# Moving two input norms to GpSimd on transposed data, in a hybrid encoder layer

## The chip, the cores and the metric

The kernel runs on one core of one Trainium2 chip. The metric is the device time of one execution in microseconds (us); lower is better. A core has a matmul engine (PE, TensorE), which loads its stationary operand with separate instructions (PEld), and three engines for element-wise work: DVE (VectorE), ACT (ScalarE) and POOL (GpSimd). SP (SyncE) issues most of the DMAs. Each engine takes its instructions in order.

## The reference

One layer of an encoder on 512 tokens of width 1024 in float32, with a memory of 256 tokens. Only the start of it matters here:

```
h = rmsnorm(x, pre_mix_g)                       # x * rsqrt(mean(x^2) + eps) * g, by row
aq, ak, av, hq, hf_fwd, hf_bwd, hi, hg = split_columns(h @ w_in, IN_SPLITS)
rec = hgrn2_group(hq, hf_fwd, hf_bwd, hi, hg, ...)     # 4 heads, a gated recurrence
...
m = rmsnorm(mem, mem_norm_g)
x = x + rmsnorm(memory_cross_attention(h, m, ...), ...)
```

Behind it come the grid attention on aq, ak and av, an output projection, the cross-attention into m, and a gated MLP with a small convolution. Each of the two norms above is a factor r by row (1/rms) and a gain g by column.

## The kernel before, in words

All matrix products are float32 made of three products of rounded parts: each operand is split into a part hi (rounded to the matmul's format, ACT writes it) and a remainder lo (DVE writes it, or POOL for 14 units), and `mm3` (L134) does hi·hi, hi·lo and lo·hi, lines 135 to 137. The weights come as 132 units of 128x1024, each loaded by SP (L110), cast by ACT (L102, out `wh`) and subtracted by DVE (L103, out `wl`). There are two buffers for raw units and four for split ones, so a load waits until the subtraction two units before it has been done, and a cast until PE has finished with the unit four before it. `unit` takes one and has up to three more issued ahead.

The order is written by hand as Python generators. `weave` advances that stream whose cost so far, divided by its share, is the smallest. Within this order a compile-time planner places the instructions on each engine by its own estimate of when their inputs will be there; each engine then runs its list in order. `tc.issue_after(i)` puts the instructions of a block that run on the engine of `i` behind `i`.

The start runs so. x comes twice: transposed (`xt`, 8 chunks of 128 features by 512 tokens) and by rows (`xr`). The first projection (the recurrence's values, L365) and head 0's three projections work on the raw transposed x times the gain (`split_x`, L335 and L336, into `raw_act`), as r is not known yet. ACT squares the rows (L378), POOL makes r (L153, L154), POOL writes four diagonal matrices of it (L382), PE multiplies them with ones (L385), and ACT copies the result (L387) to `r_bc`, which holds r along the tokens on every partition. Head 0's results are multiplied by `r_bc` on DVE (L435). Meanwhile `normalize` makes the normalised activation `hT`, chunk by chunk: DVE writes x·g·r (L392), ACT casts it and DVE subtracts (L102 and L103 with out `big`).

From there on everything reads `hT`. `mix_projections` begins with the memory's norm: loads of the gain and of the memory's rows on POOL's queue, squares on ACT (L188), r on POOL (L153, L154), scaling on DVE (L170). Then it does the gate projection (`put_sg`), heads 1 and 2 (`hgrn_in`), the memory's 16 transposes (`mem_turn`, L179, with four casts and four subtractions), keys and values, queries, and head 3. It is woven with `cores`, the recurrence of heads 0 to 2, whose first step is a sum on DVE (L486) and a matmul (L489), followed by level after level of ACT copies (L496), matmuls (L499) and DVE multiplies (L525). The shares are 100 and `CORE_SHARE` = 53, in which a step of the gate projection is 6 matmuls and costs 6 x 0.216 = 1.296. Large buffers (`big`) come from one pool of 16.

Of the kernel before, what the change touches and what calls it, by code (L numbers as in the profile page):

```python
# [18 lines left out]
P = 128  # L19
D = 1024  # L20
T = 512
NB = T // P
KC = D // P
M = 256
MB = M // P
# [6 lines left out]
TURN_STEP, MEM_TURN, UP_TURN = 0, (0, 4), (0, 2)  # L32
POOL_UNITS = frozenset(range(28, 42))
CORE_SHARE = 53.0
WARM = 4
LEVELS = (1, 2, 4, 8, 16, 32, 64)
ASK = 3
MIX_ORDER = (0, 2, 3, 1)
# [34 lines left out]
def layer(tc, io, out):  # L73
    nc = tc.nc
    ctx = ExitStack()
    pool = lambda name, **k: ctx.enter_context(tc.tile_pool(name=name, **k))
    const = pool("const", bufs=1)
# [20 lines left out]
    def tmp4(shape, dt=F32):  # L98
        return t4.tile(shape, dt, name="tmp4", tag="tmp4")

    def split(hi, lo, src, eng=None):
        nc.scalar.copy(hi, src)  # L102
        (eng or nc.vector).tensor_sub(lo, src, hi.bitcast(F32))  # L103
# [35 lines left out]
    def blk(b):  # L139
        return slice(b * P, (b + 1) * P)  # L140
# [4 lines left out]
    def gains(*names, eng=None):  # L145
        g = big([P, 2, D])
        for i, name in enumerate(names):
            (eng or nc.gpsimd).dma_start(g[:, i, :], rows_bc(io[name], D))
        return [g[:, i, :] for i in range(len(names))]

    def rstd_of(ss, n, width):
        r = small()
        nc.gpsimd.tensor_scalar(r[:, :n], ss, 1.0 / width, EPS, op0=ALU.mult, op1=ALU.add)  # L153
        last_pow[0] = nc.gpsimd.tensor_tensor(out=r[:, :n], in0=r[:, :n], in1=nhalf[:, :n], op=ALU.pow).ins  # L154
        return r
# [13 lines left out]
    def scale_rows(xb, r, g, h, c):  # L169
        nc.vector.scalar_tensor_tensor(out=h[:, half(c)], in0=xb[:, half(c)], scalar=r, in1=g[:, half(c)],  # L170
                                       op0=ALU.mult, op1=ALU.mult)

    def turn_in(h, act, b, tags, before=None):
        for c in range(2):
            if before:
                before(c)
            o = bank(tags[c]).rearrange("p (k n) -> p k n", k=4)
            for k in range(4):
                nc.tensor.transpose(o[:, k, :], h[:, blk(c * 4 + k)], ident)  # L179
            hi, lo = act.hi, act.lo  # L180
            if len(hi) == 2:
                split(hi[c][:, :, blk(b)], lo[c][:, :, blk(b)], o)
            else:
                split(hi[0][:, c * 4:c * 4 + 4, blk(b)], lo[0][:, c * 4:c * 4 + 4, blk(b)], o)

    def row_rstd(xb, h):
        ss = small()
        nc.scalar.activation(h, xb, ACT.Square, accum_out=ss[:, 0:1])  # L188
        return rstd_of(ss[:, 0:1], 1, D)[:, 0:1]
# [57 lines left out]
    def proj_tm(act, tags, use, n=512):  # L247
        o = [bank(t) for t in tags]
        nk = 1024 // n
        for j in range(8 // nk):  # L250
            w = unit(nk)
            for b in range(len(tags)):
                for k in range(nk):
                    kc = nk * j + k
                    mm3(o[b][:, :n], act.get(kc, blk(b)), (w[0][:, k, :], w[1][:, k, :]), kc == 0, kc == 7)
                if kc == 7:
                    use(b, o[b])
                yield 3 * nk * MM * n / 512
# [39 lines left out]
            pass  # L298

    ident = const.tile([P, P], F32, name="ident")  # L300
    gcol = const.tile([P, KC], F32, name="gcol")
    ones = const.tile([P, P], F32, name="ones")
    nhalf = const.tile([P, 16], F32, name="nhalf")
    warm = tmp2()
    xt = [big([P, 4, T]) for _ in range(2)]
    nc.scalar.dma_start(gcol, io["gx"])
    nc.gpsimd.memset(ones, 1.0)
    nc.vector.memset(warm[:, :256], 0.0)
    nc.gpsimd.memset(nhalf, -0.5)

    def load_xt(kc, n):
        nc.sync.dma_start(xt[kc // 4][:, kc % 4:kc % 4 + n, :], io["xt"][:, kc:kc + n, :])
# [15 lines left out]
    raw_act = new_act()  # L328

    after = []  # L330

    def split_x(kc):
        src = xt[kc // 4][:, kc % 4, :]
        hi, lo = raw_act.get(kc, slice(0, T))
        cast = nc.scalar.mul(hi, src, gcol[:, kc:kc + 1]).ins  # L335
        rest = nc.vector.scalar_tensor_tensor(out=lo, in0=src, scalar=gcol[:, kc:kc + 1], in1=hi.bitcast(F32),  # L336
                                              op0=ALU.mult, op1=ALU.subtract).ins
        return cast, rest
# [11 lines left out]
    v_ps = [bank(t) for t in "soso"]  # L350
    xr = room_x()
    ws = []
    for j in range(4):
# [7 lines left out]
        for k in range(2):  # L361
            kc = 2 * j + k
            for a, w in ((0, wh), (0, wl), (1, wh)):
                for b in range(NB):
                    nc.tensor.matmul(v_ps[b], raw_act.get(kc, blk(b))[a], w[:, half(k)],  # L365
                                     start=kc == 0 and a == 0 and w is wh, stop=kc == 7 and a == 1)
# [3 lines left out]
    ident_r = const.tile([P, P], F32R, name="ident_r")  # L370
    nc.vector.tensor_copy(ident_r, ident)
    taken[0] = 4
    for _ in range(2):
        issue()

    rx = const.tile([P, 2 * NB], F32, name="rx")
    for b in range(NB):
        nc.scalar.activation(tmp4([P, D]), xr[b], ACT.Square, accum_out=rx[:, b:b + 1])  # L378
    r = rstd_of(rx[:, :NB], NB, D)
    diag_r = tmp2((P, NB, P), tag="th")  # L380
    for b in range(NB):
        nc.gpsimd.tensor_scalar(diag_r[:, b, :], ident, r[:, b:b + 1], None, op0=ALU.mult)  # L382
    r_ps = bank("c")
    for b in range(NB):
        nc.tensor.matmul(r_ps[:, blk(b)], ones, diag_r[:, b, :], start=True, stop=True)  # L385
    r_bc = big([P, T])
    nc.scalar.copy(r_bc, r_ps)  # L387
    hT = new_act()

    def normalize(kc):  # L390
        t = tmp2()
        nc.vector.scalar_tensor_tensor(out=t, in0=xt[kc // 4][:, kc % 4, :], scalar=gcol[:, kc:kc + 1], in1=r_bc,  # L392
                                       op0=ALU.mult, op1=ALU.mult)
        split(*hT.get(kc, slice(0, T)), t)

    masks = const.tile([P, len(LEVELS), P], U8, name="masks")
    masks_f = tmp4([P, len(LEVELS), P])
# [29 lines left out]
    sg_box, heads, qkv, rec_done = [], {}, {}, [0]  # L427

    def put_v(b, o):
        nc.scalar.mul(v[:, b, :], o, r[:, b:b + 1])  # L430

    def scaled(put):
        def use(o):
# [15 lines left out]
    def hgrn_in(h, between=(), raw=False):  # L449
        qk = big([P, 2, 2, T])  # L450
        tt = big([P, 2048])
        q = tmp2(tag="tq")

        def put_q(z):
            nc.scalar.activation(q, z, ACT.Sigmoid)
            nc.vector.tensor_mul(q, z, q)

        def put_f(d):
            def put(z):
                f = tt[:, d * T:(d + 1) * T]  # L460
                k = qk[:, 1, d, :]
                nc.scalar.activation(f, z, ACT.Sigmoid)
                nc.scalar.activation(k, z, ACT.Sigmoid, scale=-1.0)
                nc.vector.tensor_scalar(f, f, oml[:, d, h:h + 1], lb[:, d, h:h + 1], op0=ALU.mult, op1=ALU.add)
# [162 lines left out]
    kv = {}  # L627

    def mem_norm():
        g_mem, = gains("mem_norm_g")  # L630
        kv["rows"] = big([P, MB, D])
        for b in range(MB):
            m = kv["rows"][:, b, :]
            nc.gpsimd.dma_start(m, io["mem"][blk(b), :])
            r = row_rstd(m, tmp4([P, D]))
            for c in range(2):
                scale_rows(m, r, g_mem, m, c)

    def mem_turn():
        kv["m"] = Act([big([P, 8, M], F32R)], [big([P, 8, M], F32R)])  # L640
        for b in range(MB):
            turn_in(kv["rows"][:, b, :], kv["m"], b, "bb")

    def mix_projections():
        mem_norm()
        yield from proj_tm(hT, tm_tags, put_sg)
        yield from hgrn_in(1)
        yield from hgrn_in(2)
        mem_turn()
        yield from proj_tm(hT, tm_tags, put_kv, 256)  # L650
        late = []
        yield from proj_tm(hT, tm_tags, lambda b, z: late.append(lambda: put_qn(b, z)))
        yield from hgrn_in(3, late)

    def cores():
        for h in range(3):
            yield from hgrn_core(h)

    for b in range(NB):
        put_v(b, v_ps[b])  # L660
    for i, _ in enumerate(hgrn_in(0, raw=True)):
        if i < KC:
            normalize(i)
    weave((mix_projections(), 100.0), (cores(), CORE_SHARE))

    kT, vv, qT = qkv["kT"], qkv["vv"], qkv["qT"]
# [340 lines left out]
```

## Time and profile before

| | |
|---|---|
| runs, us | 849.77, 849.8, 851.0; median 849.8 |
| profiled execution | 851.05 us, of it the span 849.3 us |
| mean granted clock of PE | 0.996 |
| busy in the span | PE 828.8, DVE 526.6, ACT 401.1, POOL 95.9 us |
| PE's longest stops | 5.60 us before 61.17, 1.55 before 206.91, 1.41 before 254.19, 1.37 before 6.38 |
| time to landing, weight units | 3.3 us, median of 131 |

The page lists each engine's busy time, then the span in 40 slices, then the DMA queues, then the chain of work that ended last, then the costliest groups of instructions. A line of a group reads: source line, engine, operation, out<-in with sizes, count, and then busy us, mean ns of one, and the engine's idle time ahead of them with what ended it. In a listing in order of time the first column is the start, the second the duration; in brackets stands the idle time before it and what released it.

### The profile page before, as it was taken

The numbers are of one execution on the slowest core, as the hardware profiler recorded it, in microseconds if no ns is written. First come the engines' busy times: TensorE is split into PE (matmuls) and PEld (weight loads), VectorE is DVE, ScalarE is ACT, GpSimd is POOL, SyncE is SP. The second block draws the span as 40 slices with busy tenths as digits, with TensorE's granted clock in tenths as the row PEclk, the third lists the DMA queues.
The fourth block names the chain that finished last, engine by engine and source line by source line (L and its number), as shares of the span: only waits on it lengthen the run. The fifth ranks groups of instructions, "written<-read, shape, count | busy, mean of one in ns | idle before, by whom it ended". The sixth has DMA issues, their size and how long they took to land.

```text
span 849.3 us, 11048 instructions
## 1 busy us (share of the span) xinstructions
PE 828.8 (98%) x4304; PEld 702.9 (83%) x4304; DVE 526.6 (62%) x799; ACT 401.1 (47%) x710; POOL 95.9 (11%) x128
## 2 busy tenths in 40 slices
PE   8979999999999999999999999999999999999996
PEld 6868888887889888888888998888888888888885
DVE  5598497969997774854443865555555557722224
ACT  6563345445878884644543643333333335511121
POOL 0311100224243301300001300000000000000001
PEclk9999999999999999999999999999999999999999
DMA  9722202122222224252312242223233332322212
GB/s 323 232 76 75 74 25 87 51 76 75 75 75 91 78 81 175 75 174 75 100 50 75 76 135 98 95 94 100 100 100 99 100 100 79 101 96 97 100 49 100
DMA packets 24756, 83.52 MB, mean 98 GB/s; under 512 B 3264, under 2 KB 3904, under 8 KB 24704
## 3 DMA queue, kind: packets, MB, share of 16 engines
q1 hardware_dynamic: 22752, 77.44, 27.5%
q0 software_dynamic: 1232, 4.46, 1.7%
q10 hardware_dynamic: 720, 0.92, 0.3%
q8 instruction: 34, 0.56, 0.3%
q14 instruction: 18, 0.15, 0.1%
HBM read 80.71 MB, written 2.10 MB: 98 GB/s over the span
## 4 chain that ended last, share of the span: by engine, by line
PE 87%; DVE 6%; DMA 3%; ACT 2%; issue 1%; POOL 0%; POOLq 0%; DVEq 0%; ACTq 0%
PE ps_b L135 9%; PE ps_b L136 9%; PE ps_b L137 9%; PE ps_s L137 6%; PE ps_s L135 6%; PE ps_s L136 6%; PE ps_o L135 6%; PE ps_o L137 6%; PE ps_o L136 6%; PE ps_c L135 4%; PE ps_c L136 4%; PE ps_c L137 4%; PE ps_c L499 3%; DMA raw<-in_w_dram 2%; PE ps_o L717 2%; DVE big L525 1%
## 5 line engine op out<-in xcount | busy, mean ns | idle before, releaser
L103 DVE TENSOR_TENSOR wl<-raw,wh 128x1024 fp32r<-128x1024 f32 x114 | 139.4, 1223 | 219.7 <-ACT wh L102 219.6
L102 ACT CAST wh<-raw 128x1024 fp32r<-128x1024 f32 x128 | 134.6, 1052 | 243.5 <-PE ps_o L137 80.5
L135 PE MATMUL ps_b<-big,wh 128*128 128x512 f32 (+1 forms) x320 | 118.0, 369 | 0.0
L136 PE MATMUL ps_b<-big,wh 128*128 128x512 f32 (+1 forms) x320 | 116.6, 364 | 0.0
L137 PE MATMUL ps_b<-big,wl 128*128 128x512 f32 (+1 forms) x320 | 116.5, 364 | 0.0
L137 PEld LDWEIGHTS ps_b<-big,wl 128*128 128x128 f32 x320 | 60.3, 188 | 9.3
L135 PEld LDWEIGHTS ps_b<-big,wh 128*128 128x128 f32 x320 | 60.4, 189 | 9.1
L136 PEld LDWEIGHTS ps_b<-big,wh 128*128 128x128 f32 x320 | 60.4, 189 | 8.9
L163 POOL TENSOR_SCALAR small<-small 128x1 f32<-128x1 f32 x40 | 14.0, 350 | 440.6 <-ACT tmp L194 421.7
L135 PE MATMUL ps_s<-wh,big 128*128 128x512 f32 (+1 forms) x140 | 53.8, 384 | 0.0
L137 PE MATMUL ps_s<-wh,big 128*128 128x512 f32 (+1 forms) x140 | 53.4, 382 | 0.0
L136 PE MATMUL ps_s<-wl,big 128*128 128x512 f32 (+1 forms) x140 | 52.9, 378 | 0.0
L525 DVE TENSOR_TENSOR big<-big 128x512 f32<-128x512 f32 x64 | 49.8, 786 | 2.7 <-PE ps_c L499 1.6
L135 PE MATMUL ps_o<-wh,big 128*128 128x512 f32 (+1 forms) x124 | 47.5, 383 | 0.0
L137 PE MATMUL ps_o<-wh,big 128*128 128x512 f32 (+1 forms) x124 | 47.3, 381 | 0.0
L136 PE MATMUL ps_o<-wl,big 128*128 128x512 f32 (+1 forms) x124 | 47.1, 380 | 0.0
L103 DVE TENSOR_TENSOR big<-ps_o,big 128x512 fp32r<-128x512 f32 x52 | 35.8, 688 | 15.9 <-ACT big L102 15.5
L103 POOL TENSOR_TENSOR wl<-raw,wh 128x1024 fp32r<-128x1024 f32 x14 | 33.9, 2424 | 57.9 <-ACT wh L102 49.2
L102 ACT CAST big<-ps_o 128x512 fp32r<-128x512 f32 x52 | 30.4, 585 | 19.9 <-PE ps_o L814 7.5
L135 PE MATMUL ps_b<-wh,big 128*128 128x512 f32 x92 | 36.6, 398 | 0.0
L136 PE MATMUL ps_b<-wl,big 128*128 128x512 f32 x92 | 36.1, 392 | 0.0
L137 PE MATMUL ps_b<-wh,big 128*128 128x512 f32 x92 | 36.0, 391 | 0.0
(246 smaller groups left out, 1891.7 us busy)
## 6 DMA issues: line engine op xcount, KB each, us to landing
raw<-in_w_dram SPq DMA_DIRECT2D x131, 512.0 KB, 3.3
big<-in_x_dram SPq DMA_DIRECT2D x8, 512.0 KB, 7.3
big<-in_xt_dram SPq DMA_DIRECT2D x3, 512.0 KB, 8.0
big<-in_mem_dram POOLq DMA_DIRECT2D x2, 512.0 KB, 9.4
out_dram<-big SPq DMA_DIRECT2D x4, 256.0 KB, 2.1
out_dram<-big ACTq DMA_DIRECT2D x3, 256.0 KB, 2.1
big<-in_xt_dram SPq DMA_DIRECT2D x2, 256.0 KB, 3.4
raw<-in_w_dram SPq DMA_DIRECT2D x2, 256.0 KB, 4.0
```

Source lines behind the costliest of these rows:

```text
L102: nc.scalar.copy(hi, src)
L103: (eng or nc.vector).tensor_sub(lo, src, hi.bitcast(F32))
L135: nc.tensor.matmul(o, a[0], b[0], start=start, stop=False)
L136: nc.tensor.matmul(o, a[0], b[1], start=False, stop=False)
L137: nc.tensor.matmul(o, a[1], b[0], start=False, stop=stop)
L163: nc.gpsimd.tensor_scalar(ss[:, i + 4:i + 5], ss[:, i:i + 1], 1.0 / D, ss[:, i + 3:i + 4] if i else EPS, op0=ALU.mult, op1=ALU.add)
L499: nc.tensor.matmul(o[:, b, :], kc[:, blk(b)], pat(qk, b * P, [[2 * m, P // (2 * m)], [T + m, 2], [1, m]]), start=True, stop=True)
L525: nc.vector.tensor_tensor(out=c, in0=c, in1=pat(tt, toff + off, [[2, npair], [gap, 2], [0, m]]), op=ALU.mult)
L717: nc.tensor.matmul(o, vv[:, c, h // 4].rearrange("p a d -> p (a d)"), pt[:, j, c, :], start=c + j == 0, stop=c == 3 and j == 1)
```

## The change

- The first instruction of ACT that needs a table is now a copy of a constant (`nhalf`) into a small tile.
- The second of two weight units issued ahead of the norm is now issued behind the copy of `r_bc` on ACT. The four diagonal matrices of r are written by DVE.
- `normalize` is gone. POOL multiplies the transposed x by `r_bc` in place, in four instructions of two chunks, and `hT` is then made by `split_x`, with the gain in ACT's cast and DVE's remainder as for the raw x.
- The memory's norm moves from the head of `mix_projections` to between heads 1 and 2. The host hands over the memory transposed too. Rows and transposed data are loaded, two 1 MB loads on POOL's queue. ACT squares the rows; r goes through two diagonal matrices (POOL), a matmul with ones and an ACT copy; POOL multiplies the transposed memory by it in two instructions of 128x1024. `job` then makes hi (ACT) and lo (DVE) with the gain, one chunk of 128x256 behind each of the first eight steps of the key and value projection. `mem_turn` with its 16 transposes is gone, as is the load of the gain by rows: the gains of x and memory come as one small table by feature.
- `cores` begins by yielding `CORE_LEAD` = 3.0.

```diff
-WARM = 4
+WARM, CORE_LEAD = 4, 3.0
...
-    gcol = const.tile([P, KC], F32, name="gcol")
+    gcol = const.tile([P, 2 * KC], F32, name="gcol")
...
+    table = small()
+    nc.scalar.copy(table, nhalf)
...
-    def split_x(kc):
+    def split_x(kc, act=raw_act):
         src = xt[kc // 4][:, kc % 4, :]
-        hi, lo = raw_act.get(kc, slice(0, T))
+        hi, lo = act.get(kc, slice(0, T))
...
-    for _ in range(2):
-        issue()
-
-    rx = const.tile([P, 2 * NB], F32, name="rx")
+    issue()
+
+    rx = small()
...
-        nc.gpsimd.tensor_scalar(diag_r[:, b, :], ident, r[:, b:b + 1], None, op0=ALU.mult)
+        nc.vector.tensor_scalar(diag_r[:, b, :], ident, r[:, b:b + 1], None, op0=ALU.mult)
...
-    nc.scalar.copy(r_bc, r_ps)
+    spread = nc.scalar.copy(r_bc, r_ps).ins
+    with tc.issue_after(spread):
+        issue()
     hT = new_act()
-
-    def normalize(kc):
-        t = tmp2()
-        nc.vector.scalar_tensor_tensor(out=t, in0=xt[kc // 4][:, kc % 4, :], scalar=gcol[:, kc:kc + 1], in1=r_bc,
-                                       op0=ALU.mult, op1=ALU.mult)
-        split(*hT.get(kc, slice(0, T)), t)
+    for i in range(4):
+        two = xt[i // 2][:, 2 * (i % 2):2 * (i % 2) + 2, :]
+        nc.gpsimd.tensor_tensor(out=two, in0=two, in1=r_bc[:, None, :].to_broadcast([P, 2, T]), op=ALU.mult)
...
     def mem_norm():
-        g_mem, = gains("mem_norm_g")
-        kv["rows"] = big([P, MB, D])
+        gm = gcol[:, KC:]
+        mt, rows = big([P, KC, M]), big([P, MB, D])
+        nc.gpsimd.dma_start(rows, io["mem"].rearrange("(b p) d -> p b d", p=P))
+        nc.gpsimd.dma_start(mt, io["mt"])
+        ss = small()
         for b in range(MB):
-            m = kv["rows"][:, b, :]
-            nc.gpsimd.dma_start(m, io["mem"][blk(b), :])
-            r = row_rstd(m, tmp4([P, D]))
-            for c in range(2):
-                scale_rows(m, r, g_mem, m, c)
-
-    def mem_turn():
+            nc.scalar.activation(tmp4([P, D]), rows[:, b, :], ACT.Square, accum_out=ss[:, b:b + 1])
+        r = rstd_of(ss[:, :MB], MB, D)
+        diag = tmp2((P, MB, P), tag="th")
+        for b in range(MB):
+            nc.gpsimd.tensor_scalar(diag[:, b, :], ident, r[:, b:b + 1], 1.0, op0=ALU.mult, op1=ALU.mult)
+        o = bank("b")[:, :M]
+        for b in range(MB):
+            nc.tensor.matmul(o[:, blk(b)], ones, diag[:, b, :], start=True, stop=True)
+        wide = tmp2((P, M), tag="th")
+        nc.scalar.copy(wide, o)
+        for c in range(2):
+            part = mt[:, 4 * c:4 * c + 4, :]
+            nc.gpsimd.tensor_tensor(out=part, in0=part, in1=wide[:, None, :].to_broadcast([P, 4, M]), op=ALU.mult)
         kv["m"] = Act([big([P, 8, M], F32R)], [big([P, 8, M], F32R)])
-        for b in range(MB):
-            turn_in(kv["rows"][:, b, :], kv["m"], b, "bb")
+
+        def job(kc):
+            hi, lo = kv["m"].get(kc, slice(0, M))
+            nc.scalar.mul(hi, mt[:, kc, :], gm[:, kc:kc + 1])
+            nc.vector.scalar_tensor_tensor(out=lo, in0=mt[:, kc, :], scalar=gm[:, kc:kc + 1], in1=hi.bitcast(F32),
+                                           op0=ALU.mult, op1=ALU.subtract)
+        return job
 
     def mix_projections():
-        mem_norm()
         yield from proj_tm(hT, tm_tags, put_sg)
         yield from hgrn_in(1)
+        split_m = mem_norm()
         yield from hgrn_in(2)
-        mem_turn()
-        yield from proj_tm(hT, tm_tags, put_kv, 256)
+        for kc, step in enumerate(proj_tm(hT, tm_tags, put_kv, 256)):
+            if kc < KC:
+                split_m(kc)
+            yield step
...
     def cores():
+        yield CORE_LEAD
         for h in range(3):
             yield from hgrn_core(h)
...
     for i, _ in enumerate(hgrn_in(0, raw=True)):
         if i < KC:
-            normalize(i)
+            split_x(i, hT)
```

More of the change, by code (lines that the diff above doesn't have):

```diff
@@ L429, in put_v @@
     def put_v(b, o):
-        nc.scalar.mul(v[:, b, :], o, r[:, b:b + 1])
+        return nc.scalar.mul(v[:, b, :], o, r[:, b:b + 1]).ins
     def scaled(put):
@@ L659, in layer @@
     for b in range(NB):
-        put_v(b, v_ps[b])
+        v_out = put_v(b, v_ps[b])
     for i, _ in enumerate(hgrn_in(0, raw=True)):
         if i < KC:
-            normalize(i)
+            split_x(i, hT)
     weave((mix_projections(), 100.0), (cores(), CORE_SHARE))
@@ L987 @@
     arrays["xt"] = a["x"][0].reshape(T, KC, P).transpose(2, 1, 0)
-    arrays["gx"] = a["pre_mix_g"][0].reshape(KC, P).T
+    arrays["gx"] = np.concatenate([a[n][0].reshape(KC, P).T for n in ("pre_mix_g", "mem_norm_g")], axis=1)
     del arrays["pre_mix_g"]
+    arrays["mt"] = a["mem"][0].reshape(M, KC, P).transpose(2, 1, 0)
+    del arrays["mem_norm_g"]
     arrays["hg_lb"] = a["hg_lb"].reshape(2, 2, 4, P).transpose(3, 0, 1, 2)
```

## The prediction

> **What bounds the kernel now.** I read the page's head, then the busy times by stretch to find where the matmul engine is not full, then the instructions in order of time at those places.
>
> ```profile
> span 849.3 us, 11048 instructions
> PE 828.8 (98%) x4304; PEld 702.9 (83%) x4304; DVE 526.6 (62%) x799; ACT 401.1 (47%) x710; POOL 95.9 (11%) x128
> 40.00:60.00 20.00, 15.56 (x69) 12.57 (x67) 16.27 (x25) 13.81 (x20) 3.17 (x4) 1.00 0.27 86
> 140.00:160.00 20.00, 19.68 (x151) 18.45 (x150) 19.55 (x42) 9.70 (x20) 2.15 (x4) 1.00 0.17 53
> ```
>
> PE is busy for 98% of the span, so the change can pay only where PE idles, or by taking work off it. (A stretch's columns are its length, then PE, weight loads, DVE, ACT and POOL busy.) PE lacks 4.4 us between 40 and 60, and next to nothing between 140 and 160, although DVE is almost full there. The profiled execution took 851.05 us, its span and 1.75 us around it; the median of the runs, 849.8, lies 1.25 below it. I make the sum in the span and take the difference off the median. Less than 0.2% (1.7 us) cannot be told from no change.
>
> The first place is the start.
>
> ```profile
> 3.81 1.28 ACT L335 ACT_TABLE_LOAD   x1 [3.81 <-DMA big<-in_xt_dram]
> 5.10 0.72 ACT L335 ACTIVATE big<-big,gcol 128x512 fp32r<-128x512 f32 x1
> 5.73 0.60 ACT L341 CAST wh<-raw 128x512 fp32r<-128x512 f32 x1
> 6.38 0.79 PE L365 MATMUL ps_s<-wh,big 128*128 128x512 f32 x1 [1.37 <-ACT wh L341]
> gcol<-in_gx_dram ACTq DMA_DIRECT2D x1, 4.0 KB, 3.2
> ```
>
> ACT loads its table only when the first x has landed: 1.28 us between data and work, and PE waits 1.37 us for the cast behind it.
>
> The second place is larger.
>
> ```profile
> 47.02 0.39 PE L135 MATMUL ps_s<-wh,big 128*128 128x512 f32 x1
> 55.18 0.39 PE L135 MATMUL ps_o<-wh,big 128*128 128x512 f32 x1
> 61.17 2.08 PE L489 MATMUL ps_c<-tmp,tmp 128*128 128x128 f32 x8 [5.60 <-DVE tmp L486]
> 63.03 1.77 PE L499 MATMUL ps_c<-big,tmp 128*128 128x128 f32 x8
> 66.15 1.20 PE L499 MATMUL ps_c<-big,tmp 128*128 128x128 f32 x8
> 214.89 1.16 PE L489 MATMUL ps_c<-tmp,tmp 128*128 128x128 f32 x8 [1.09 <-DVE tmp L486]
> ```
>
> PE leaves head 0's input projection at 47.02, does 37 matmuls of the gate projection (36 spacings of 0.227 us make the 8.16 us to 55.18), and then stands for 5.60 us: next in its queue is the first matmul of the recurrent core, L489. What follows is slow: L489 takes 2.08 us, where the same group behind a stop of 1.09 took 1.16, and L499 takes 1.77 where a later one takes 1.20. These add 0.9 and 0.6, so the stop costs 5.6 + 1.5 = 7.1 us.
>
> The Trainium skill, in "TensorE: Matmul & The Clock Gate", Part 1, says that the array falls to half its clock after an idle window of some 3.4 us. The trace agrees: slow behind 5.60, not slow behind 1.09.
>
> Why the core was late is in the chain of waits, with the waits and the DMA table beside it.
>
> ```profile
> 32.63 8.67 DMA raw<-in_w_dram
> 54.50 1.05 ACT tmp L188 x2
> 55.63 0.93 POOL small L153
> 59.10 1.41 DVE big L170 x2
> 60.51 0.61 DVE tmp L486
> raw<-in_w_dram SPq DMA_DIRECT2D x131, 512.0 KB, 3.3
> ACT wh L102 <- DMA raw<-in_w_dram: 8.3, 3, 3.7
> ```
>
> Two things add up. One weight load lands after 8.67 us where the median of 131 is 3.3; ACT waits up to 3.7 us for such a load, and DVE falls behind with it. Then the memory's norm (L188, L153, L170) stands in DVE's queue directly ahead of the core's first step, L486.
>
> **The change part by part. The table.** The copy of a constant has its input before ACT has anything else to do, so the load goes beside the first transfers. L335 then starts when the gains land (issue at 0.72 and 3.2 = 3.92, rounded to 4.0), the cast 0.63 later and PE 0.65 after that, at 5.28: 1.1 us earlier. PE then shows no idle time up to 55.57, so all of this moves, as long as its data keep ahead of it.
>
> **The spread of r.** Four small multiplies go from POOL to DVE. Either way they lie behind the first projection, at whose end, 29.77, their matmuls start:
>
> ```profile
> 24.00 2.91 POOL L382 TENSOR_SCALAR tmp<-ident,small 128x128 f32<-128x128 f32 x4
> 29.77 1.05 PE L385 MATMUL ps_c<-tmp,ones 128*128 128x128 f32 x8
> 30.58 0.48 PE L135 MATMUL ps_b<-big,wh 128*128 128x512 f32 x1
> 33.23 0.58 ACT L387 COPY big<-ps_c 128x512 f32<-128x512 f32 x1
> 25.48 1.05 ACT L102 CAST wh<-raw 128x1024 fp32r<-128x1024 f32 x1 [2.06 <-DMA raw<-in_w_dram]
> ```
>
> They end at 26.91, with 2.9 us to spare; without that cover they would cost PE at most those 2.9. The copy L387 came at 33.23, behind casts that waited for loads. The change puts it ahead of one weight unit's cast, which was at 25.48: the copy from 29.7 to 30.3, the cast to 31.35. The unit's load keeps its place on SP's queue, and only ACT's part waits. Queued behind it are the other casts on ACT and this unit's subtraction on DVE. PE asks for the unit 24 matmuls (5.4 us) after 30.58 - 1.1, at 34.9. The subtraction, 1.22 us by a row below, ends at 32.6 if nothing holds it: 2.3 us to spare, so I cost this at nothing.
>
> **x normalised by GpSimd, and the memory's norm out of the way.** Eight multiplies L392 leave DVE and POOL does the same in four of 128x1024 from 30.3 on; hT's casts and remainders stay on ACT and DVE. The memory's norm with its four L170 goes behind head 1's projection. These rows price it (groups of DVE from 30 to 61, a stretch, and two instructions that overlapped):
>
> ```profile
> L392 DVE SCALAR_TENSOR_TENSOR tmp<-big,gcol 128x512 f32<-128x512 f32 x8 | 5.7, 743 | 0.0
> L170 DVE SCALAR_TENSOR_TENSOR big<-big,small 128x512 f32<-128x512 f32 x4 | 2.8, 748 | 1.2 <-POOL small L154 1.2
> L103 DVE TENSOR_TENSOR wl<-raw,wh 128x1024 fp32r<-128x1024 f32 x5 | 6.1, 1221 | 5.2 <-ACT wh L102 5.2
> 31.30:61.10 29.80, 24.27 (x107) 19.73 (x106) 24.96 (x37) 19.26 (x30) 3.19 (x5) 1.00 0.42 141
> L103 POOL TENSOR_TENSOR wl<-raw,wh 128x1024 fp32r<-128x1024 f32 x14 | 33.9, 2424 | 57.9 <-ACT wh L102 49.2
> 201.97 2.40 POOL L103 TENSOR_TENSOR wl<-raw,wh 128x1024 fp32r<-128x1024 f32 x1 [0.28 <-ACT wh L102]
> 202.43 2.23 DVE L464 TENSOR_SCALAR big<-big,oml,lb 128x512 f32<-128x512 f32 x1 [0.31 <-ACT big L462]
> L464 DVE TENSOR_SCALAR big<-big,oml,lb 128x512 f32<-128x512 f32 x2 | 1.1, 540 | 0.0
> ```
>
> From 31.3 to the end of L486 DVE works 24.96 us and idles 4.84. The change leaves 24.96 - 5.7 - 2.8 and adds the delayed subtraction, 1.22: 17.7 us. DVE starts on it at 31.35, so L486 ends at 49.05 + X, where X is what holds or starves DVE.
>
> X has two parts. Idle: 4.84 less the 1.2 that went with L170 is 3.64, between 0 (if the late load goes, its rivals for the DMA engines having moved) and 3.64; I take half, 1.8. Holds: a POOL multiply of this size takes 2.42 us, and L464, which takes 0.54 elsewhere, took 2.23 when it started inside one and ended 0.29 after it. Each of the four can therefore hold DVE by 1.69, as in that row, up to its whole length: 0 to 4 x 2.42 less the 1.05 that pass before DVE's first subtraction, 8.6. I take two of the four at 1.69, 3.4, because DVE also has work on PSUM and waits of its own to lay beside them. X is 5.2, and L489 can start at 54.3.
>
> The Trainium skill, in "SBUF — State Buffer", section "Who interferes with whom", says that a DVE instruction with two SBUF inputs and a GpSimd one that reads SBUF exclude each other for a whole instruction. The L464 row agrees. By that rule alone, with every multiply in DVE's way, the sum would be that of the rival on the port below.
>
> **The lead.** The weave advances the gate projection by 1.296/100 per step of six matmuls and the core by its cost over 53; a lead of 3.0 lets five such steps go first, 30 matmuls, where by the code's order one did. (The trace shows 37 ahead of L489, so the order made at compile time departs from the code's by what it expects to be ready.) I count 30: PE reaches L489 at 47.02 - 1.1 + 6.8 = 52.7, and stands 1.6 us until 54.3. At L489 the kernel is 61.17 - 54.3 = 6.9 us earlier with 7 matmuls (1.6 us) less behind it: 5.3 gained, the 1.1 of the start within it. The slow matmuls go too, since 1.6 is nearer to 1.09 than to 5.60: 1.5. Next late is then DVE itself, by the core's own steps.
>
> **The memory's transposes.** Sixteen go, in four groups; two matmuls with ones come. (Order of time, and the DMA table.)
>
> ```profile
> 142.76 0.60 PE L179 MATMUL ps_b<-ident,big 128*128 128x128 f32 x4
> 143.12 0.36 PE L137 MATMUL ps_o<-wh,big 128*128 128x256 f32 x1
> 143.32 0.28 PE L135 MATMUL ps_o<-wh,big 128*128 128x256 f32 x1
> big<-in_mem_dram POOLq DMA_DIRECT2D x2, 512.0 KB, 9.4
> ```
>
> A group delays the next matmul by 0.36, and that one takes 0.08 more to the one after it (0.20 against the 0.12 that the 0.28 rows keep): 0.44 a group, 1.76 us. Four L385 took 30.58 - 29.77 = 0.81, so two cost 0.4. PE gains 1.3. On DVE, eight half-size remainders replace four subtractions at about the same sum, and two more POOL multiplies can hold it for 0 to 4.8 us; PE shows no stop near 140 with DVE 98% busy, so I take 0 and keep 4.8 in mind for the range. The memory's loads (now 1 MB each, in two orders, with no gain broadcast) move on POOL's queue past x's multiplies.
>
> The sum is 5.3 + 1.5 + 1.3 = 8.1 us of span, or **841.7 us** from the median.
>
> **The rivals.** *Nothing is left of the stop*: X at or below 3.6. For it: the late load's cause moves away, and of the DVE work some can be ordered behind L486. Then 61.17 - 52.7 - 1.6 = 6.9, with 1.5 and 1.3: 9.7, 840.1 us. The cold matmuls at the very start (0.43 apart at first against 0.227) might also shorten as the 1.37 us of idle shrinks; as a bound I allow 1.5 as behind the stop, 838.6.
>
> *The port takes it all back*: all four multiplies stand in DVE's way, X = 8.6 + 1.8 = 10.4, L489 at 59.5. For it: nearly all that DVE has there reads SBUF twice. Against: POOL is only one of the things DVE waits for, and the waits overlap. Left are 61.17 - 59.5 - 1.6 = 0.1, the slow clock stays, and 1.3: 848.4 us, within the 0.2%.
>
> *The memory's chain stops PE instead*, and the kernel is slower. The two matmuls with ones stand in PE's queue behind a load (9.4 us by its row, for half the size), two squares (2 x 1.05), the rstd (2 x 0.93) and two multiplies on POOL (2.91 / 2). If PE reaches them as the load is issued, it stands for 14.9 us and pays 1.5 for the clock: 841.7 + 16.4 = 858.1 us. It decides from a stop of 9.8 us on; below that the gain is only eaten. For it: just such a chain, L188 to L489, made the present stop. Against: the load depends on no computation, only on a free buffer, and head 1's projections give it time.
>
> *The change doesn't do what it says at the start*: the copy's table is another than the one that L335 needs, and the load stays at 3.81. Only one load was needed for the scaled copy, but a copy alone could choose otherwise. 841.7 + 1.1 = 842.8 us.
>
> **How the numbers follow.** The forecast gets 0.40, nothing left 0.27, the port 0.17, the memory's chain 0.09, the table 0.07. The range from 838.5 to 848.5 takes in the start's bound below and the port above; it leaves out the chain and some of the port's tail. Faster: 0.40 + 0.27 + 0.07 and 0.07 of the port, 0.81; the other 0.10 of the port is no change; slower is the chain, 0.09.
>
> **What would show it.** Right: the table load begins before the first x lands and PE's first L365 is near 5.3; the stop ahead of L489 is under 3 us, and its group takes about 1.2; DVE instructions of over 1.5 us stand inside POOL's four multiplies; no L179 near 140 us, and no stop at the two matmuls with ones. Wrong: a stop of 5 us or more at L489 (the port, or a load that is still late), a PE wait released by POOL or by the copy of the memory's r, or a new stop between 60 and 140 us.

## The result, and the profile after

| | before | after |
|---|---|---|
| median, us | 849.78 | 862.53 |
| runs, us | 849.26 to 851.0 (4) | 862.13 to 864.68 (4) |
| profiled execution: span, us | 849.3 | 862.0 |
| mean granted clock of PE | 0.996 | 0.991 |
| PE's stops over 0.12 us, sum | 13.5 | 22.9 |

The changed kernel is slower: ratio 1.0153, 95% interval 1.0133 to 1.0173, or 12.7 us more. The forecast was 841.7 us, with 0.81 on faster. One run of lead0, an experiment below, took 2133 us where its other three lie between 856.16 and 857.4; it is left out of that version's median and ratio.

First the head of the page, then three stretches (length, then PE, weight loads, DVE, ACT and POOL busy, with the granted clock as the third number from the end).

```profile
span 862.0 us, 11016 instructions
PE 832.4 (97%) x4292; PEld 705.4 (82%) x4292; DVE 536.6 (62%) x795; ACT 403.8 (47%) x716; POOL 111.4 (13%) x129
```

```profile
40.00:60.00 20.00, 15.23 (x58) 12.10 (x57) 19.67 (x25) 11.31 (x15) 2.98 (x2) 0.83 0.35 118
120.00:140.00 20.00, 18.34 (x101) 15.88 (x102) 15.89 (x24) 6.83 (x11) 0.43 (x1) 0.91 0.13 40
220.00:240.00 20.00, 18.07 (x122) 16.69 (x123) 19.27 (x35) 15.14 (x29) 5.12 (x2) 0.91 0.22 75
```

PE still lacks over 4 us between 40 and 60, now at a granted clock of 0.83, where it had 1.00. Two more stretches have 0.91; before, one had (60 to 80). The span grew by 12.7: stops give 9.4, the clock some 4.4 ((1 - 0.991) x 862.0 less (1 - 0.996) x 849.3); the prediction's 1.3 for the saved matmuls comes off, which makes 12.5.

PE's stops up to 125 us, from the list in order of time, with L489, where the old stop was (two small ones, of 0.56 before 81.69 and 0.65 before 88.72, are left out):

```profile
5.61 0.79 PE L367 MATMUL ps_s<-wh,big 128*128 128x512 f32 x1 [0.59 <-ACT wh L343]
46.07 0.76 PE L135 MATMUL ps_b<-big,wh 128*128 128x512 f32 x1 [4.77 <-DVE tmp L435]
60.50 1.05 PE L489 MATMUL ps_c<-tmp,tmp 128*128 128x128 f32 x8
107.81 0.50 PE L135 MATMUL ps_s<-wh,big 128*128 128x256 f32 x2 [0.91 <-ACT wh L102]
109.07 0.39 PE L136 MATMUL ps_s<-wl,big 128*128 128x256 f32 x1 [0.53 <-DVE wl L103]
113.04 0.84 PE L643 MATMUL ps_b<-tmp,ones 128*128 128x128 f32 x4 [1.45 <-POOL tmp L640]
121.66 1.67 PE L499 MATMUL ps_c<-big,tmp 128*128 128x128 f32 x8 [3.24 <-DVE big L525]
```

The stop at L489 is gone, as forecast. In its place PE stands 4.77 us at a point that the prediction didn't look at: head 0's last projection, which needs a bank `b` of PSUM, the memory that PE writes its results to, and L435 on DVE has not yet emptied it. Three small stops and one of 3.24 lie around the memory's norm. A third group follows behind 195 us, small stops of up to 1.6: 8.2 us in all, where before it was 4.6.

What DVE and POOL did ahead of the first large stop:

```profile
31.11 11.87 POOL L394 TENSOR_TENSOR big<-big 128x1024 f32<-128x1024 f32 x4 [2.95 <-ACT big L388]
32.01 2.59 DVE L103 TENSOR_TENSOR wl<-raw,wh 128x1024 fp32r<-128x1024 f32 x1 [3.05 <-ACT wh L102]
35.26 2.68 DVE L103 TENSOR_TENSOR wl<-raw,wh 128x1024 fp32r<-128x1024 f32 x1 [0.66 <-ACT wh L102]
37.87 6.32 DVE L338 SCALAR_TENSOR_TENSOR big<-big,gcol 128x512 fp32r<-128x512 f32 x3
44.11 1.21 DVE L103 TENSOR_TENSOR wl<-raw,wh 128x1024 fp32r<-128x1024 f32 x1
45.25 0.68 DVE L435 TENSOR_TENSOR tmp<-ps_b,big 128x512 f32<-128x512 f32 x1
```

POOL's four multiplies (L394) last from 31.11 to 42.98. In that time two L103 take 2.59 and 2.68 and three L338 6.32 us (2.89, 2.84 and, behind POOL's last multiply, 0.74); the next L103, after POOL's end, takes 1.21. L435 stands behind all of them in DVE's queue; where nothing held DVE (the first experiment) it ran at 39.19. The chain is: POOL holds DVE, DVE reaches L435 late, the bank comes free late, PE stops. The Trainium skill, in "SBUF — State Buffer", section "Who interferes with whom", states the exclusion; these rows agree, and they add who pays in the end, which is PE.

The memory's two multiplies, 70 us later, show the same:

```profile
98.06 0.96 POOL L632 DMA_DIRECT2D big<-in_mem_dram  x1
112.22 1.12 POOL L640 TENSOR_SCALAR tmp<-ident,small 128x128 f32<-128x128 f32 x2
114.37 5.49 POOL L648 TENSOR_TENSOR big<-big,tmp 128x1024 f32<-128x1024 f32 x2 [1.03 <-ACT tmp L645]
115.08 2.67 DVE L525 TENSOR_TENSOR big<-big 128x512 f32<-128x512 f32 x1 [2.05 <-ACT tmp L496]
117.60 2.29 DVE L530 TENSOR_TENSOR big<-big 128x8 f32<-128x8 f32 x1
```

L530 on 8 columns takes 2.29 us here, while two of it on 16 columns take 0.35 together at 66.52, where POOL is idle: its time is that of a POOL instruction and not its own. These two are steps of the recurrent core, so L499 on PE waits.

### The profile page after: what moved, and what is told of

Read it like the earlier page. It is cut to its first block, busy times and chain, and to the rows that moved or that the text cites. A ratio compares the mean times of both kernels' runs of the same rounds, so it can differ in the third digit from the quotient of the medians.

```text
span 862.0 us, 11016 instructions
## 1 busy us (share of the span) xinstructions
PE 832.4 (97%) x4292; PEld 705.4 (82%) x4292; DVE 536.6 (62%) x795; ACT 403.8 (47%) x716; POOL 111.4 (13%) x129
## 4 chain that ended last, share of the span: by engine, by line
PE 79%; DVE 8%; ACT 2%; issue 1%; POOL 1%; POOLq 0%; DVEq 0%; ACTq 0%
PE ps_b L136 8%; PE ps_b L137 8%; PE ps_b L135 8%; PE ps_s L137 6%; PE ps_s L136 6%; PE ps_s L135 6%; PE ps_o L135 5%; PE ps_o L137 5%; PE ps_o L136 5%; PE ps_c L137 4%; PE ps_c L135 4%; PE ps_c L136 4%; DVE big L525 2%; PE ps_c L499 2%; PE ps_o L734 2%; PE ps_o L722 1%
## 5 line engine op out<-in xcount | busy, mean ns | idle before, releaser
L103 DVE TENSOR_TENSOR wl<-raw,wh 128x1024 fp32r<-128x1024 f32 x114 | 142.2, 1247 | 220.2 <-ACT wh L102 219.9
L135 PE MATMUL ps_b<-big,wh 128*128 128x512 f32 (+1 forms) x320 | 119.8, 374 | 4.8 <-DVE tmp L435 4.8
L136 PE MATMUL ps_b<-big,wh 128*128 128x512 f32 (+1 forms) x320 | 118.2, 369 | 0.0
L135 PEld LDWEIGHTS ps_b<-big,wh 128*128 128x128 f32 x320 | 61.2, 191 | 14.4 <-issue 5.2
L136 PEld LDWEIGHTS ps_b<-big,wh 128*128 128x128 f32 x320 | 61.5, 192 | 9.1
L525 DVE TENSOR_TENSOR big<-big 128x512 f32<-128x512 f32 x64 | 54.5, 861 | 10.3 <-PE ps_c L499 6.4
L103 DVE TENSOR_TENSOR big<-ps_o,big 128x512 fp32r<-128x512 f32 x52 | 35.7, 687 | 15.9 <-ACT big L102 15.5
L103 POOL TENSOR_TENSOR wl<-raw,wh 128x1024 fp32r<-128x1024 f32 x14 | 34.4, 2459 | 62.5 <-ACT wh L102 48.9
L499 PE MATMUL ps_c<-big,tmp 128*128 128x128 f32 x224 | 33.5, 292 | 4.7 <-DVE big L525 4.7
L499 PEld LDWEIGHTS ps_c<-big,tmp 128*128 128x128 f32 x224 | 30.8, 196 | 7.7 <-ACT tmp L496 3.6
L135 PE MATMUL ps_b<-wh,big 128*128 128x512 f32 x92 | 36.6, 398 | 0.0
```

What stands on the lines that cost most here:

```text
L135: nc.tensor.matmul(o, a[0], b[0], start=start, stop=False)
L136: nc.tensor.matmul(o, a[0], b[1], start=False, stop=False)
L499: nc.tensor.matmul(o[:, b, :], kc[:, blk(b)], pat(qk, b * P, [[2 * m, P // (2 * m)], [T + m, 2], [1, m]]), start=True, stop=True)
L525: nc.vector.tensor_tensor(out=c, in0=c, in1=pat(tt, toff + off, [[2, npair], [gap, 2], [0, m]]), op=ALU.mult)
```

## The experiments

Two theories stood after the result. **The port**: POOL's six multiplies hold DVE, and PE pays through banks and core steps. **The order**: the lead of 3.0 and the moved norm give a worse order of work, and the multiplies matter little. Ratios below are to the kernel before, run on the same chip, with the 95% interval in brackets. Differences in us are between medians of different groups of runs; the kernel before itself lies between 849.78 and 850.65 in them, so a difference of less than 1 us says nothing.

### Port or order

*x_dve: the changed kernel with x's four multiplies on DVE.*

```diff
-        nc.gpsimd.tensor_tensor(out=two, in0=two, in1=r_bc[:, None, :].to_broadcast([P, 2, T]), op=ALU.mult)
+        nc.vector.tensor_tensor(out=two, in0=two, in1=r_bc[:, None, :].to_broadcast([P, 2, T]), op=ALU.mult)
```

> The changed kernel, but the four multiplies of the transposed x by r run on DVE instead of POOL; nothing else. Port theory (POOL's multiplies hold DVE's two-input instructions, DVE then frees PSUM late and PE stops 4.8 us at 46 us and runs 3.4 us slow after it): the stop at 46 us goes, DVE's 2.6 us subtractions near 32 and 35 us go back to 1.2, some of the gain is lost to a stop ahead of L489 because DVE now does the multiplies itself; about 857 us. Order theory (the loss comes from the instruction order that the moved memory norm and the lead bring, not from POOL): within 1.5 us of 862.5.

Measured: 856.18 us, 1.0071 [1.0045, 1.0098]: 6.3 better than the changed kernel. DVE's list at the same place:

```profile
30.39 1.22 DVE L103 TENSOR_TENSOR wl<-raw,wh 128x1024 fp32r<-128x1024 f32 x1
31.53 3.49 DVE L394 TENSOR_TENSOR big<-big 128x1024 f32<-128x1024 f32 x3
39.19 0.68 DVE L435 TENSOR_TENSOR tmp<-ps_b,big 128x512 f32<-128x512 f32 x1
```

DVE now does more work and is done sooner: L435 starts at 39.19 instead of 45.25, and PE doesn't stop there. The 3.2 us at the memory remains.

*mem_dve: the changed kernel with the memory's two multiplies on DVE.*

```diff
-            nc.gpsimd.tensor_tensor(out=part, in0=part, in1=wide[:, None, :].to_broadcast([P, 4, M]), op=ALU.mult)
+            nc.vector.tensor_tensor(out=part, in0=part, in1=wide[:, None, :].to_broadcast([P, 4, M]), op=ALU.mult)
```

> The changed kernel, but the two multiplies of the transposed memory run on DVE instead of POOL; nothing else. Port theory: the DVE instructions of 2.7 and 2.3 us near 115 and 118 us go back to about 0.7 and 0.2, the PE stop of 3.2 us at 121.7 us shrinks to under 1.5 and the slow clock behind it goes; about 858 us. Order theory: within 1.5 us of 862.5, with the 1.45 us stop at the matmuls with ones and the waits near 108 us still there under both.

Measured: 859.0 us, 1.0099 [1.008, 1.0117]: 3.5 better. In DVE's list the two multiplies take 2.36 us together, where POOL took 5.49:

```profile
115.16 2.36 DVE L648 TENSOR_TENSOR big<-big,tmp 128x1024 f32<-128x1024 f32 x2 [1.58 <-ACT tmp L645]
117.43 2.14 DVE L525 TENSOR_TENSOR big<-big 128x512 f32<-128x512 f32 x2
```

L499 no longer stops PE there; the stop near 46 stays, at 4.78.

*both_dve: both edits, all six multiplies on DVE.*

> The changed kernel with both sets of multiplies on DVE. Port theory: the two gains add, about 853 us, so still a little slower than the kernel before because of what the moved memory norm costs. Order theory: about 861 us.

Measured: 850.79 us, 1.0009 [1.0, 1.0019], lower than either theory had it. The two edits together are worth 11.7 us. Alone they gave 6.3 and 3.5; the 1.9 between is less than the interval of the first allows (2.2 us to each side).

*lead0: the changed kernel without its lead.*

```diff
     def cores():
-        yield CORE_LEAD
```

> The changed kernel without the lead of 3.0 for the cores; nothing else. Port theory: the stop at 46 us lies ahead of the cores and stays, L489 comes earlier in PE's queue and waits for DVE there; within 3 us of 862.5, either way. Order theory (the lead pushes the cores' DVE work into the attention stage, whose stops after 200 us grew from 4.6 to 8.2 us): faster by 3 to 5 us, with the stops after 200 us back near 4.6.

Measured: 857.03 us, 1.0081 [1.0064, 1.0097]: 5.5 better. The stops behind 195 us fall from 8.2 to 4.6; both stops from POOL stay (4.78 and 3.23). So neither theory does alone: the port costs more, and the lead is a second loss, which the prediction had counted as a gain.

### Do the losses add up, and what of the memory's chain

*both_dve_lead0: both edits and no lead.*

> The changed kernel with all six multiplies on DVE and without the lead. If the losses add (port 11.7 us, lead 5.3 us as each measured alone): 845.5 us, with the PE stops after 200 us back near 4.6 us in all. Rival: the lead only hurt because POOL had already delayed PE; with DVE doing the multiplies the core's first matmul comes before its input again, a stop of 3 to 6 us at L489 near 55 us appears, and the time stays at 850 to 852.

Measured: 845.3 us, 0.9949 [0.9934, 0.9963], the lowest of all versions, though three others below lie within 1 us of it. The losses add up. What is left of the change is 5 us of gain. In the profiles PE's stops sum to 10.9 us (before 13.5), its clock is 0.999 (before 0.996), and L489 starts at 52.02 with no stop. Against it stand the small stops at the memory, of which the second row is the largest:

```profile
52.02 1.05 PE L489 MATMUL ps_c<-tmp,tmp 128*128 128x128 f32 x8
103.22 0.84 PE L643 MATMUL ps_b<-tmp,ones 128*128 128x128 f32 x4 [1.42 <-POOL tmp L640]
```

*both_dve_lead0_s: the same, with the memory's sum in another PSUM bank.* The thought was that bank `b` made the planner take key and value matmuls ahead of head 2's, before their weights were ready.

```diff
-        o = bank("b")[:, :M]
+        o = bank("s")[:, :M]
```

> As the kernel before this one, and the sum over the memory's r takes a PSUM bank that head 2's projections do not need (s for b). Bank theory: the bank held for the two matmuls with ones keeps head 2 from starting, PE takes the first part of the key and value projection early and waits for its weights (0.9 and 0.5 us) and then for POOL (1.4 us); with the other bank head 2's matmuls fill that time, and 1.5 to 2.8 us go: 843 to 844 if the one before gives 845.5. Rival: the two matmuls stand at the same place in PE's queue, so the wait for POOL stays or grows; no gain.

Measured: 845.85 us, 0.9954 [0.9934, 0.9974]. The waits of 0.91 and 0.53 go, but these rows stand in PE's list:

```profile
105.50 0.84 PE L643 MATMUL ps_s<-tmp,ones 128*128 128x128 f32 x4 [1.59 <-POOL tmp L640]
135.28 0.30 PE L553 MATMUL ps_c<-ident,tmp 128*128 128x128 f32 x1 [1.30 <-DVE tmp L549]
```

The wait for POOL stays and another appears. The bank is not what costs.

*early: both_dve_lead0 with the memory's norm ahead of head 1's projection.*

```diff
-        yield from hgrn_in(1)
         split_m = mem_norm()
+        yield from hgrn_in(1)
```

> All multiplies on DVE and no lead, with the memory's norm taken up ahead of head 1 instead of behind it. If the memory chain is late because its loads and squares are taken up late (load issued near 98 us): the wait for POOL at the two matmuls with ones (1.4 us) and the waits for the weights of the early key and value part (0.9 and 0.5 us) go, 842 to 844. Rival: the loads wait for free buffers, not for their turn in the order, so nothing moves, or a stop at the cores comes back; 845 to 849.

Measured: 848.62 us, 0.9983 [0.9973, 0.9993], 3.3 worse than without the edit. PE stops 3.18 us earlier on, for DVE, at the end of core 0:

```profile
83.55 1.10 PE L553 MATMUL ps_c<-ident,tmp 128*128 128x128 f32 x4 [3.18 <-DVE tmp L549]
```

Of the two places, the one between heads 1 and 2 is the better.

*memold_lead0: the kernel before with the table, the spread of r and x on POOL, as in the change; the memory's norm is the old one, and there is no lead.* The core of the edit:

```diff
+    nc.scalar.copy(table, nhalf)
...
+    with tc.issue_after(spread):
+        issue()
...
-    def normalize(kc):
...
+        nc.gpsimd.tensor_tensor(out=two, in0=two, in1=r_bc[:, None, :].to_broadcast([P, 2, T]), op=ALU.mult)
...
-            normalize(i)
+            split_x(i, hT)
```

> As the kernel before this one, but x's four multiplies on POOL as in the change. Port theory: as in the changed kernel PE stops some 4.8 us in head 0's last projection and runs slow behind it, 5 to 8 us more than with DVE doing them. Order theory: no difference beyond 1.5 us.

*xdve_memold_lead0: the same with `nc.vector` for `nc.gpsimd` in x's multiplies.*

> The kernel before with the early table load, the split of x normalised in place by DVE, and the copy of r ahead of a cast; the memory's norm by rows at its old place with its 16 transposes, and no lead. Theory that the memory norm ahead of the cores made the stop at L489: the stop of 5 us stays, and the time is 848 to 851. Rival (the late weight load and DVE's backlog made it): the stop is under 2.5 us and the time is near 845.

Measured: 850.79 us, 1.0012 [1.0001, 1.0023], with PE's stop at L435 (4.78 at 44.69); and 847.16 us, 0.9971 [0.9957, 0.9985], with no stop at L489. The port's price is 3.6 here, less than the 5 to 8 expected. The pair says little on the memory's norm as a cause of the stop at L489, because the order came out otherwise than in the source (the second kernel's DVE list):

```profile
54.28 0.69 DVE L486 TENSOR_TENSOR tmp<-big 128x512 f32<-128x512 f32 x1
58.24 1.41 DVE L170 SCALAR_TENSOR_TENSOR big<-big,small 128x512 f32<-128x512 f32 x2 [0.75 <-POOL small L154]
```

The planner put the norm's scaling behind the core's first step. L486 starts 6.1 us earlier than in the kernel before (60.43). Two things changed at once: the norm is out of the way, and ACT waits less for weight loads. From 20 to 62 us that wait is, in the kernel before,

```profile
ACT wh L102 <- DMA raw<-in_w_dram: 10.4, 4, 3.7
```

(total, times, longest), and in this one

```profile
ACT wh L102 <- DMA raw<-in_w_dram: 3.1, 1, 3.1
```

Which of the two ended the stop is open.

### How much of the port, and the small parts alone

*x_half: both_dve_lead0 with the second and fourth of x's multiplies on POOL.*

```diff
-        nc.vector.tensor_tensor(out=two, in0=two, in1=r_bc[:, None, :].to_broadcast([P, 2, T]), op=ALU.mult)
+        (nc.vector, nc.gpsimd)[i % 2].tensor_tensor(out=two, in0=two, in1=r_bc[:, None, :].to_broadcast([P, 2, T]), op=ALU.mult)
```

> All multiplies on DVE and no lead (845.3 us), but POOL takes the second and fourth of x's four multiplies. Port theory, by dose: a POOL multiply holds DVE for up to its length, so two of them cost about half of what four cost (four cost 3.6 us beside the old memory norm and 6 to 8 us in the changed kernel); the stop in head 0's last projection is between 0 and 2.5 us: 846 to 849. Rival (only the back-to-back run of four hurts, single ones are hidden): no difference beyond 1 us, or a little faster, as DVE has two multiplies less.

Measured: 850.54 us, 0.9997 [0.9985, 1.0008]: two POOL instructions cost 5.2 us (850.54 - 845.3), more than expected. POOL, DVE and PE in order of time:

```profile
29.20 6.78 POOL L394 TENSOR_TENSOR big<-big 128x1024 f32<-128x1024 f32 x2 [1.33 <-DMA raw<-in_w_dram]
30.30 3.43 DVE L103 TENSOR_TENSOR wl<-raw,wh 128x1024 fp32r<-128x1024 f32 x1
33.65 3.41 DVE L394 TENSOR_TENSOR big<-big 128x1024 f32<-128x1024 f32 x1
42.07 0.47 PE L135 MATMUL ps_b<-big,wh 128*128 128x512 f32 x1 [2.68 <-DVE tmp L435]
43.08 0.63 PE L135 MATMUL ps_b<-big,wh 128*128 128x512 f32 x1
```

Two DVE instructions of 1.2 us each take 3.4, and each side waits for the other: POOL's pair takes 6.78 instead of the 4.8 that two need alone. PE stops for 2.68 and its next matmuls take 0.63 instead of 0.39. So the price is not in proportion to POOL's work: all four cost 6.3 by x_dve, 8.2 by mem_dve less both_dve, and 3.6 beside the old memory norm. Not all of the 5.2 is shown to come from the hold: in the profiled execution the clock is 0.91 from 40 to 60, behind the stop, but again from 200 to 220, long after POOL's two multiplies; both_dve_lead0 has 1.00 in both.

*table: the kernel before with the early table load alone.*

```diff
+    table = small()
+    nc.scalar.copy(table, nhalf)
```

> The kernel before with the early table load alone. By the changed kernel's start (first matmul of the first projection at 5.61 instead of 6.38 us) it is worth 0.8 us if the stop at L489 lets it through; that stop is set by DVE and the late weight load, so it may swallow it: 849 to 850.5.

Measured: 850.64 us, 1.0 [0.999, 1.001]. The start is earlier, but PE loses it at L489 (this row's line number is two higher for the two added lines):

```profile
60.78 2.08 PE L491 MATMUL ps_c<-tmp,tmp 128*128 128x128 f32 x8 [6.82 <-DVE tmp L488]
```

The stop has grown from 5.60 by 1.2: a gain ahead of a stop counts only if what ends the stop moves too.

### The lead

*lead_only: the kernel before with the lead alone.*

```diff
     def cores():
+        yield 3.0
```

> The kernel before with the lead of 3.0 for the cores alone. The compile-time order leaves L489 where it was (37 matmuls of the gate projection ahead of it), so the stop ahead of it stays. Theory that the lead costs by itself, by pushing the cores' steps toward the attention stage: 3 to 6 us slower, 853 to 856, with longer stops after 200 us. Rival: it costs only beside the moved memory norm; within 1.5 us of 850.

Measured: 859.52 us, 1.0106 [1.009, 1.0121]: 9.2 us, more than expected. The stop at L489 stays (4.57 at 61.51), so the lead gains next to nothing where it was meant to. Behind 195 us the stops are 9.5 instead of 4.6. The largest of them, and the stretch around it:

```profile
222.39 0.89 PE L706 MATMUL ps_o<-ident,tmp 128*128 128x128 f32 x4 [2.02 <-ACT tmp L682]
```

```profile
220.00:240.00 20.00, 15.54 (x106) 14.21 (x105) 17.64 (x37) 13.45 (x28) 5.31 (x2) 0.91 0.18 58
```

In the kernel before, the same stretch has 19.37 us of PE at a clock of 1.00. What is late shows in one row for the transposes at the end of each core (L553, from 80 to 210 us, which holds the three cores of the weave; minimum, median and maximum of one in ns, then first and last start), first the kernel before, then this one:

```profile
L553 PE MATMUL ps_c<-ident,tmp x12: 270/272/319, 94.6 to 184.2; 128*128 128x128 f32 x12
```

```profile
L553 PE MATMUL ps_c<-ident,tmp x12: 270/272/273, 102.2 to 190.0; 128*128 128x128 f32 x12
```

Core 0 ends 7.6 us later, and the last of the three still 5.8.

*lead_s57: the lead, with the cores' share raised to 57.*

```diff
-CORE_SHARE = 53.0
+CORE_SHARE = 57.0
```

> The kernel before with the lead of 3.0 and the cores' share raised from 53 to 57, so that lead and cores together end where the cores ended without a lead (45/57 against 42/53 of the projections). If the lead costs because the cores end late: most of the 9.2 us comes back, 850 to 853. If the order of the weave matters in no regular way: still 857 to 861.

Measured: 853.64 us, 1.0038 [1.0025, 1.005]: 5.9 of the 9.2 come back, and the stops behind 195 us are 4.6 again. The three cores' ends, in the same view, the last now 1.9 us later than in the kernel before:

```profile
L553 PE MATMUL ps_c<-ident,tmp x12: 270/272/273, 100.4 to 186.1; 128*128 128x128 f32 x12
```

*both_dve_s57: both edits, lead kept, share 57.*

> The changed kernel with all multiplies on DVE, lead of 3.0 kept, share 57. If the lead costs because the cores end late: near the 845.3 of the one without a lead, at most 847. Otherwise near the 850.8 with lead and share 53.

Measured: 845.57 us, 0.9942 [0.9925, 0.9958], equal to the version without a lead (845.3). All that the lead cost is back. The third core's last transpose starts at 178.3 here, at 177.8 without a lead and at 183.1 with the lead and a share of 53.

*lead1: the kernel before with a lead of 1.0. both_dve_lead1: both edits with a lead of 1.0.*

> The kernel before with a lead of 1.0. If the cost follows the size: about 3 us, 853. If it is a matter of one order or another: either no cost or the full 9 us.

> The changed kernel with all multiplies on DVE and a lead of 1.0. If the cost follows the size: about 1.8 us over the 845.3 without a lead, 847. Otherwise 845 or 851.

Measured: 854.05 us, 1.0048 [1.0031, 1.0064], or 3.4 above the kernel before; and 846.22 us, 0.9944 [0.993, 0.9959], 0.9 above 845.3. On the kernel before the price follows the size of the lead; with both edits the 0.9 is no difference, and shows only that a lead of 1.0 costs far less than the 5.5 of 3.0. That the delay of the cores is the cause is supported from two sides: a smaller lead and a larger share both give time back, and the cores' ends move with it. No run has the share of 57 without a lead, so a gain of the share by itself is not excluded. Why the delay hurts is argued, not shown: the stops come behind 195 us, after the three cores have ended, where DVE still has the queries to do beside the grid attention and is 88 to 97% busy from 200 to 240 in both kernels; no run took that work away. Why the same lead costs 9.2 on the kernel before and 5.5 on the changed one, with POOL's multiplies or without, is open.

## Why the prediction was wrong, step by step

- **The table: right in kind.** The load starts at 1.16 us, beside the first transfers, and PE's first L367 is at 5.61, 0.77 earlier than before; forecast 1.1.
- **"PE then shows no idle time up to 55.57, so all of this moves": failed.** It held for the kernel before. The prediction looked for the new wait only at L489, where the old one was, and not at each point where PE needs something from DVE on the way. Such a point lies at 41 us: the bank that L435 empties.
- **"Two of the four at 1.69, 3.4": half of what it was.** DVE's five instructions under POOL's multiplies took 5.27 + 6.32 = 11.6 us. Unheld they are 2 x 1.22 + 2.07 = 4.5 (three L338 in a row take 2.07 in x_half). The holds are 7.1 us, twice the term and below its bound of 8.6. The size of one hold was near (1.8 on average, against 1.69); the count was not, as each of POOL's four multiplies held one instruction. L464, the row that the size came from, reads one tensor and two columns of scalars, so it was no instance of the rule on two inputs beside it; L103, L338 and L525 are. The reason given, that DVE has work on PSUM to lay beside them, didn't apply: in that stage the planner had five instructions in a row that read SBUF twice.
- **Memory multiplies, "I take 0": failed.** No stop near 140 was the wrong row: it spoke of the old place, where POOL did nothing of this kind. The new place holds steps of the core on DVE. Cost: a stop of 3.24 and slow matmuls behind it, 3.5 us by mem_dve.
- **The port in sum.** The prediction's terms were 3.4 and 0. Undoing both moves to POOL brings 11.7 us, and as much without a lead (857.03 - 845.3). The rival on the port gave 848.4, because it too placed the whole cost at L489, where at most the old stop could return, with one slow clock; it did not count PE stopping in a new place and again at the memory.
- **The lead, counted as 30 matmuls of cover: failed, also in sign.** With the multiplies on DVE, no cover is needed: without a lead L489 starts at 52.02 with no stop. The prediction followed the lead up to L489 and no further. It delays all three cores and costs 5.5 us here (lead0), 9.2 alone.
- **The slow clock behind a stop: right, and then used on one place only.** Stops of 4.77 and 3.24 were followed by clocks of 0.83 and 0.91 in their stretch. In x_half 2.68 was enough: seven matmuls behind it take 0.63 instead of 0.39. The Trainium skill's page "TensorE: Matmul & The Clock Gate", Part 1, puts the idle window at some 3.4 us; the stops here say less, and the measurement decides.
- **The memory's chain: right in kind.** L643 waits 1.45 us for POOL, far from the 9.8 from which it would decide.
- **Transposes: right.** No L179 is left, and PE has 12 instructions fewer (16 transposes against four passes of the matmuls with ones).

The sum, then, runs so: without the port and the lead the change is worth -5.0 us (845.3 against 850.3); the port adds 11.7 and the lead 5.5 (both_dve less both_dve_lead0). That is 12.2, against 12.7 measured.

## What to carry to other kernels

Before moving element-wise work from DVE to POOL, look at DVE's neighbours in time. Where they read two tensors from SBUF, as here, one DVE instruction pays for each POOL instruction, and PE can pay at the first bank or step that waits behind it in DVE's queue. Price such a move by listing every point at which PE takes something from DVE until the end of the stage, and not only the stop that is to be removed. A head start for one of two woven streams is a delay of the other for as long as both run: follow it to the stage where the late one ends, and give the share back if the head start is kept.

## What the runs showed of the hardware

- POOL and DVE alternated, one instruction each. Four POOL multiplies of 128x1024 took 2.42, 3.40, 3.39 and 2.81 us, 11.87 from first to last (the first, which started while DVE was idle, took what such an instruction takes by the earlier rows), and beside them four DVE instructions took 2.59, 2.68, 2.89 and 2.84. Two POOL multiplies took 6.78; a DVE instruction's width hardly mattered for its wait (2.29 us for 128x8, 2.67 for 128x512).
- The same two 128x1024 multiplies took 2.36 us on DVE and 5.49 on POOL.
- A slow clock doesn't need one long stop: between 220 and 240 the changed kernel was granted 0.91, with no stop over 1.2 us in the stretch and one of 1.64 at its edge (219.88). The kernel before had stops of 1.55 and 1.09 between 200 and 220, at 1.00. What separates the two is open. Executions of one kernel differ in it as well: x_dve's four had mean clocks of 0.998, 0.992, 0.995 and 0.994, and took 853.53, 857.33, 855.04 and 858.4 us.
